# One product of 512 columns for two of 256 in the expert inputs of a float32 decoder step

## The chip, the cores and the metric

The kernel runs on one core of one Trainium2 chip. The metric is the device time of one execution in microseconds (us); less is better. The core has five engines: TensorE multiplies matrices (the profile shows its matmuls as PE and its weight loads as PEld), VectorE (DVE) and ScalarE (ACT) work on tiles elementwise, GpSimd (POOL) here mostly starts gathers, and SyncE (SP) starts the other transfers from memory. SBUF is the memory on the core, PSUM the memory that TensorE adds its products into; a PSUM tile here is one bank of 128 x 512 float32.

## The reference

A decoder trunk of two layers works on 256 prompt positions and 32 sample positions (8 sequences of 4), 288 rows of 1024 in all. The first layer mixes over time with RWKV-7, the second with differential attention. After each stands a "PEER" mixer, which holds this change: for every row it picks 16 experts of 16,384 for each of 8 heads, and an expert is a single neuron, one row of `u_tab` and one of `v_tab`.

```python
q = (xblk @ w_q + b_q).reshape(PEER_BLOCK, PEER_HEADS, 2, PEER_HALF)
sc = jnp.einsum('thcd,cnd->thcn', q, subkeys).astype(jnp.float32)
...
expert = i1 * PEER_NKEYS + i2
gate = jax.nn.softmax(s_sel, axis=-1)
h = jnp.einsum('td,thkd->thk', xblk, u_tab[expert])
act = (gate * jax.nn.gelu(h.astype(jnp.float32))).astype(xblk.dtype)
return jnp.einsum('thk,thkd->td', act, v_tab[expert])
```

## The kernel before, in words

For the 256 prompt rows the kernel does not gather experts: it computes all 16,384 of them, in 128 chunks of 128, and multiplies by a gate that is zero for those not picked. For the 32 sample rows it gathers the picked rows (64 gathers of 128 rows, 1 MB each).

**Split products.** Most products are taken on values split in two. ScalarE casts a float32 tile to float32r (the high part `wh`), VectorE subtracts it from the original (the low part `wl`); `split` does both, here in two halves of 512 columns. The activations have high and low parts too, `xH` and `xL` (`self.hl`), of 8 blocks `d` by 288 columns. `mm3` then makes three products for each block `d` of 128 inputs, all added into one PSUM tile: `wh` by `xH` (line 285), `wh` by `xL` (line 286), `wl` by `xH` (line 287).

**Hidden block.** `upto(n)` makes chunks of the first half of the mixer up to number n. For chunk c it loads 512 KB of `u` (transposed) into a `raw` tile, splits it (lines 263 and 264), runs `mm3` over 8 `d` on the 256 prompt columns, 24 matmuls into a PSUM tile `pu` (two such tiles take turns), and ScalarE applies the gelu from PSUM into `gel(c)` (line 1301). The first 23 chunks of a layer go another way (`direct`, line 1298): plain float32, no split, which TensorE runs as two instructions for each `d`. The 105 others of each layer take the split way.

**Output block.** The loop over c (line 1462) first calls `upto` for a few chunks ahead (line 1467: 31 chunks at the start, down to 8 ahead), then loads and splits 512 KB of `v` (`wload_rows`), multiplies gate and gelu on VectorE into `act` (line 1472), splits that into `ah` and `al`, and runs 24 matmuls (line 1491) of 256 columns into `pa`, four banks that gather the sum over all chunks. In the first part of the loop several output blocks stand between two hidden ones; from about c = 36 they alternate.

**Around them.** A gate table of half the experts is built before the loop and the other half in it, from c = 48 on: four VectorE instructions (lines 1401 to 1404), 32 small matmuls (lines 1411 and 1412) and ScalarE copies for 16 rows at a time, one such piece for each c. Between the chunks, a gather for the sample rows (line 1422) is followed by a dot product (line 1426) and a weighted sum (line 1430) on VectorE.

**Order.** The program is written chunk by chunk; a scheduler with a time model of its own arranges each engine's instructions, and each engine then works strictly in that order. Tiles named `raw` (three buffers), `wh` and `wl` (two each) are shared by hidden and output blocks in turn, so the cast for one block waits until TensorE has used the `wh` of two blocks before, and a load of `raw` waits until VectorE has subtracted the block three before.

Of the kernel before, what the change touches and what calls it, by code (L numbers as in the profile page):

```python
# [10 lines left out]
F32R = mybir.dt.float32r  # L11
# [10 lines left out]
NT, TP, TS = 288, 256, 32  # L22
# [120 lines left out]
class Yoco:  # L143
# [18 lines left out]
    def resident(self):  # L162

        p = self.ctx.enter_context(self.tc.tile_pool(name="hl", bufs=1, side="right"))
        self.xT = p.tile([128, 8, NT], F32, name="xT")
        self.ones = p.tile([128, 128], F32, name="ones")
        self.nc.gpsimd.memset(self.ones, 1.0 / 1024)
        self.one = p.tile([128, 128], F32, name="one")
        self.nc.gpsimd.memset(self.one, 1.0)
        self.alpha = p.tile([128, 128], F32, name="alpha")  # L170
        self.nc.scalar.activation(self.alpha, self.C["ident"], AF.Copy, scale=ALPHA)
        self.lnT = p.tile([128, 8, 8], F32, name="lnT")
        self.hl = p.tile([128, 8, NT], F32R, name="xH"), p.tile([128, 8, NT], F32R, name="xL")
        self.stream(self.ctx, *self.WS, "right")
        self.rp, self.att = p, None

# [102 lines left out]
    def mm3(self, ps, w, x, n, kb=8, ds=None):  # L279
        (wh, wl), (xh, xl) = w, x  # L280
        ps = ps[:, :n]
        blk = lambda t, d: t[d][:, :n] if isinstance(t, list) else t[:, d, :n]
        for d in ds or range(kb):
            h, l = wh[:, d * 128:(d + 1) * 128], wl[:, d * 128:(d + 1) * 128]
            self.nc.tensor.matmul(ps, h, blk(xh, d), start=d == 0, stop=False)  # L285
            self.nc.tensor.matmul(ps, h, blk(xl, d), start=False, stop=False)  # L286
            self.nc.tensor.matmul(ps, l, blk(xh, d), start=False, stop=d == kb - 1)  # L287

    def raw_load(self, src):

        w = self.raw()
        self.nc.sync.dma_start(w, src.rearrange("p b m -> p (b m)"))
        return w
# [965 lines left out]
    def peer(self, l, mean):  # L1259

        tc, nc, A, C = self.tc, self.nc, self.A, self.C
        V, S, T, G = nc.vector, nc.scalar, nc.tensor, nc.gpsimd
        uT, uv = A[f"uT{l}"], A[f"uv{l}"]
        with ExitStack() as es:
# [15 lines left out]
            def gel(c):  # L1280

                return early[:, c if c < A_ else (c - A_) % R_]
# [5 lines left out]
            def upto(n, direct=False):  # L1288


                while st["u"] < min(n, 128):
                    c = st["u"]
                    ps = self.psu()[:, :TP]
                    if direct:
                        w = self.raw(turn=True)
                        nc.sync.dma_start(w, uT[c].rearrange("p b m -> p (b m)"))
                        for d in range(8):
                            T.matmul(ps, w[:, d * 128:(d + 1) * 128], self.xT[:, d, :TP], start=d == 0, stop=d == 7)  # L1298
                    else:
                        self.mm3(ps, self.wload(uT[c]), self.hl, TP)  # L1300
                    S.activation(gel(c), ps, AF.Gelu_apprx_tanh)  # L1301
                    st["u"] += 1

            with tc.tile_pool(name="tk", bufs=1) as tk, ExitStack() as es2:
# [32 lines left out]
                for h in range(9):  # L1337
                    if h < 8:
                        self.proj(A[f"pq{l}"], self.hl, q_evac, ms=(2 * h, 2 * h + 1) if h else (), eng=G, pre=wq)
                    if h:  # L1340
                        for j in range(2):
                            self.tk_half(tk2, tt[j], qT, sk, h - 1)
                    upto(self.DIRECT.get(h, 0), True)
                    if h % 4 == 0 and h:
                        for j in range(2):
                            self.tk_pairs(tk2, tt[j], h - 4, 4)
                    if 1 <= h < 5:
                        self.ln_rest(4 * l, 2 * h - 2)
                        self.ln_rest(4 * l, 2 * h - 1)
                    if h == 6:  # L1350
                        with self.behind(last + after[1:]):
                            S.copy(self.io, C["iota"].unsqueeze(2).to_broadcast([128, 128, 2]))
                            S.copy(self.i16, C["iota"][:, :16].unsqueeze(2).to_broadcast([128, 16, 16]))
                            if not self.att:
                                self.attention_scalars()
                    if h == 4:
                        self.dbg(f"x1_{l}", self.xT)
                        xs4 = tk2.tile([128, 8, 4, TS], F32, name="xs4")
                        S.copy(xs4, self.xT[:, :, TP:].unsqueeze(2).to_broadcast([128, 8, 4, TS]))
                        for n in range(2):  # L1360
                            ps = self.psa()
                            for b in range(4):
                                T.transpose(ps[:, b * 128:(b + 1) * 128], xs4[:, 4 * n + b].rearrange("p r t -> p (r t)"), C["ident"])
                            S.copy(Xs[:, n * 512:(n + 1) * 512], ps)
                for j in (0, 1):
                    iw, gt = self.tk_decode(tk2, tt[j])
                    upto(self.DEC[j], True)
                    ps = self.psb()
                    ts = slice(j * 128, (j + 1) * 128)
                    for n, x in enumerate((iw[:, 0], iw[:, 1], gt.rearrange("p u k -> p (u k)"))):  # L1370
                        T.transpose(ps[:, n * 128:(n + 1) * 128], x, C["ident"])
                    S.copy(i1T[:, ts], ps[:, 0:128])
                    S.copy(i2T[:, ts], ps[:, 128:256])
                    g15 = tk2.tile([128, 128], F32, tag="g15", name=self.nm("g15"))
                    S.activation(g15, ps[:, 256:384], AF.Copy, scale=32768.0)
                    V.tensor_copy(gH[:, ts], g15)
                    V.tensor_sub(gL[:, ts], g15, gH[:, ts])
                upto(self.FIRST, True)
                self.ws = one
            self.hs = self.HG  # L1380
# [81 lines left out]
            for c in range(128):  # L1462
# [20 lines left out]
                if c == 127:  # L1483
                    ps = self.psb()[:, :TP]
                    for b in range(8):
                        T.matmul(ps[:, b * TS:(b + 1) * TS], accS[:, b * 128:(b + 1) * 128], C["rep"][:, :TS], start=True, stop=True)
                    x = self.xT[:, :, TP:]
# [9 lines left out]
            for n in range(4):  # L1497
                x = self.xT[:, 2 * n:2 * n + 2, :TP]
# [391 lines left out]
```

## Time and profile before

| | |
|---|---|
| median of three runs | 2329.24 us (2320.59 to 2331.36) |
| profiled execution | 2323.59 us |
| its span, first to last instruction | 2321.8 us |
| mean granted TensorE clock | 0.989 of full speed |
| TensorE / VectorE / ScalarE / GpSimd busy | 97% / 76% / 51% / 17% of the span |
| moved by DMA | 439.44 MB, mean 189 GB/s |

The span is the profiled execution's time from its first to its last instruction; 1.8 us lie around it. A line of instructions is named by its line of the kernel (L1491), by what it writes and reads (`pa<-ah,wh`), and by the shape; numbers behind the bar are busy us, mean ns of one, and the idle time of the engine before it with what ended it. A matmul's time in the records reaches from its start to the arrival of its result, so neighbours overlap.

### The profile page before, as it was taken

The numbers are of one execution on the slowest core, as the hardware profiler recorded it, in microseconds if no ns is written. First come the engines' busy times: TensorE is split into PE (matmuls) and PEld (weight loads), VectorE is DVE, ScalarE is ACT, GpSimd is POOL, SyncE is SP. The second block draws the span as 40 slices with busy tenths as digits, with TensorE's granted clock in tenths as the row PEclk, the third lists the DMA queues.
The fourth block names the chain that finished last, engine by engine and source line by source line (L and its number), as shares of the span: only waits on it lengthen the run. The fifth ranks groups of instructions, "written<-read, shape, count | busy, mean of one in ns | idle before, by whom it ended". The sixth has DMA issues, their size and how long they took to land. (4 is left out here: it accounts for less than half of the span.)

```text
span 2321.8 us, 49203 instructions
## 1 busy us (share of the span) xinstructions
PE 2253.4 (97%) x19296; PEld 2121.8 (91%) x19296; DVE 1759.4 (76%) x4125; ACT 1177.1 (51%) x2713; POOL 391.1 (17%) x424
## 2 busy tenths in 40 slices
PE   9989999999999999999999999999999999999998
PEld 6768889799999999999999888979999999999998
DVE  5758788977776987777785657897877797776776
ACT  3425453445455555544565666345545564554555
POOL 0323154000210210010013246100101021101101
PEclk9989999999999999999999999999999999999999
DMA  5222443245666567776746564325567656777673
GB/s 185 73 67 80 126 160 119 95 151 166 239 242 226 192 215 258 244 253 237 263 170 237 200 207 144 114 83 173 186 237 244 215 196 214 254 247 258 235 244 122
DMA packets 117624, 439.44 MB, mean 189 GB/s; under 512 B 14504, under 2 KB 18264, under 8 KB 108560
## 3 DMA queue, kind: packets, MB, share of 16 engines
q1 hardware_dynamic: 103216, 351.86, 44.8%
q0 software_dynamic: 14176, 84.44, 10.4%
q8 instruction: 151, 2.47, 0.4%
q14 instruction: 81, 0.66, 0.1%
HBM read 424.05 MB, written 5.94 MB: 185 GB/s over the span
## 5 line engine op out<-in xcount | busy, mean ns | idle before, releaser
L263 ACT CAST wh<-raw 128x512 fp32r<-128x512 f32 x1116 | 657.0, 617 | 696.0 <-PE pa L1491 223.7
L264 DVE TENSOR_TENSOR wl<-raw,wh 128x512 fp32r<-128x512 f32 x1052 | 704.0, 694 | 322.1 <-ACT wh L263 304.9
L1491 PE MATMUL pa<-al,wh 128*128 128x256 f32 x2048 | 569.7, 278 | 2.6 <-DVE al L264 2.5
L1491 PE MATMUL pa<-ah,wh 128*128 128x256 f32 x2048 | 568.1, 278 | 1.6 <-ACT ah L263 1.6
L1491 PE MATMUL pa<-ah,wl 128*128 128x256 f32 x2048 | 567.7, 277 | 0.6 <-DVE wl L264 0.4
L287 PE MATMUL pu<-xH,wl 128*128 128x256 f32 x1696 | 482.7, 285 | 15.8 <-DVE wl L264 15.0
L286 PE MATMUL pu<-xL,wh 128*128 128x256 f32 x1696 | 481.9, 284 | 0.0
L285 PE MATMUL pu<-xH,wh 128*128 128x256 f32 x1696 | 480.8, 284 | 0.9 <-ACT wh L263 0.9
L1491 PEld LDWEIGHTS pa<-al,wh 128*128 128x128 f32 x2048 | 386.1, 189 | 3.3 <-DVE al L264 3.2
L1491 PEld LDWEIGHTS pa<-ah,wh 128*128 128x128 f32 x2048 | 384.9, 188 | 2.9 <-ACT ah L263 1.8
L1491 PEld LDWEIGHTS pa<-ah,wl 128*128 128x128 f32 x2048 | 386.3, 189 | 1.2 <-DVE wl L264 1.2
L287 PEld LDWEIGHTS pu<-xH,wl 128*128 128x128 f32 x1696 | 321.4, 189 | 20.8 <-DVE wl L264 20.4
L285 PEld LDWEIGHTS pu<-xH,wh 128*128 128x128 f32 x1696 | 324.3, 191 | 1.7 <-ACT wh L263 1.5
L286 PEld LDWEIGHTS pu<-xL,wh 128*128 128x128 f32 x1696 | 323.2, 191 | 0.2 <-DVE xL L264 0.2
L285 PE MATMUL pa<-xH,wh 128*128 128x288 f32 x656 | 196.4, 302 | 0.3 <-ACT xH L263 0.3
L1422 POOL DMA_INDIRECT gt<-in_uv,ex x64 | 107.8, 1684 | 516.0 <-DVE accS L1430 489.9
L286 PE MATMUL pa<-xL,wh 128*128 128x288 f32 x656 | 193.9, 297 | 0.6 <-DVE xL L1113 0.5
L287 PE MATMUL pa<-xH,wl 128*128 128x288 f32 x656 | 192.8, 295 | 0.1
L1478 POOL COPY pace<-act 128x1 f32<-128x1 f32 x64 | 37.6, 588 | 887.8 <-DVE act L1472 846.3
L1298 PE MATMUL pu<-xT,raw 128*128 128x256 f32 x736 | 172.9, 386 | 0.0
L1298 PEld LDWEIGHTS pu<-xT,raw 128*128 128x128 f32 x736 | 136.6, 192 | 17.6 <-issue 1.0
L1301 ACT ACTIVATE gel<-pu 128x256 f32<-128x256 f32 x256 | 97.1, 379 | 75.4 <-PE pu L1298 75.2
(491 smaller groups left out, 3592.2 us busy)
## 6 DMA issues: line engine op xcount, KB each, us to landing
raw<-in_uT SPq DMA_DIRECT2D x256, 512.0 KB
raw<-in_uv SPq DMA_DIRECT2D x256, 512.0 KB
raw<-in_pq SPq DMA_DIRECT2D x32, 512.0 KB
raw<-in_wg SPq DMA_DIRECT2D x16, 512.0 KB
raw<-in_rw_w_k SPq DMA_DIRECT2D x8, 512.0 KB
raw<-in_rw_w_r SPq DMA_DIRECT2D x8, 512.0 KB
raw<-in_rw_w_v SPq DMA_DIRECT2D x8, 512.0 KB
raw<-in_rw_w_o SPq DMA_DIRECT2D x8, 512.0 KB
```

Source lines behind the costliest of these rows:

```text
L263: self.nc.scalar.copy(h, x)
L264: self.last = (eng or self.nc.vector).tensor_sub(l, x, h).ins
L285: self.nc.tensor.matmul(ps, h, blk(xh, d), start=d == 0, stop=False)
L286: self.nc.tensor.matmul(ps, h, blk(xl, d), start=False, stop=False)
L287: self.nc.tensor.matmul(ps, l, blk(xh, d), start=False, stop=d == kb - 1)
L1298: T.matmul(ps, w[:, d * 128:(d + 1) * 128], self.xT[:, d, :TP], start=d == 0, stop=d == 7)
L1301: S.activation(gel(c), ps, AF.Gelu_apprx_tanh)
L1422: G.indirect_dma_start(out=gt, out_offset=None, in_=uv, in_offset=bass.IndirectOffsetOnAxis(ap=ex[:, col:col + 1], axis=0))
L1478: with tc.issue_after(G.tensor_copy(pace, act[:, :1]).ins):
L1491: T.matmul(acc[b], w[:, b * 128:(b + 1) * 128], x, start=False, stop=c == 127 and b % 2 == 1 and w is vl)
```

## The change

The two tiles `xH` and `xL` become one tile `xHL`, in which the two parts of each `d` lie side by side; the old names are views of it. For the split hidden blocks, `mm_hidden` takes the place of `mm3`: `wh` meets the prompt columns of both parts in one product of 2 x 256 columns, which fills a whole PSUM bank (first half: sum over `xH`, second half: sum over `xL`), and `wl` by `xH` is added to the first half as before. The two halves are then added: ScalarE copies the second into `gel(c)`, VectorE adds the first to it, and the gelu works in place there.

```diff
-        self.hl = p.tile([128, 8, NT], F32R, name="xH"), p.tile([128, 8, NT], F32R, name="xL")
+        self.parts = p.tile([128, 8, 2, NT], F32R, name="xHL")
+        self.hl = self.parts[:, :, 0], self.parts[:, :, 1]
...
+    def mm_hidden(self, ps, wh, wl):
+
+
+        T, x = self.nc.tensor, self.parts
+        for d in range(8):
+            h, l = wh[:, d * 128:(d + 1) * 128], wl[:, d * 128:(d + 1) * 128]
+            T.matmul(ps.rearrange("p (n t) -> p n t", n=2), h, x[:, d, :, :TP], start=d == 0, stop=d == 7, skip_group_check=True)
+            T.matmul(ps[:, :TP], l, x[:, d, 0, :TP], start=False, stop=d == 7, skip_group_check=True)
...
-                    ps = self.psu()[:, :TP]
+                    both = self.psu()
+                    ps = both[:, :TP]
...
-                        self.mm3(ps, self.wload(uT[c]), self.hl, TP)
+                        self.mm_hidden(both, *self.wload(uT[c]))
+                        S.copy(gel(c), both[:, TP:])
+                        V.tensor_add(gel(c), ps, gel(c))
+                        ps = gel(c)
                     S.activation(gel(c), ps, AF.Gelu_apprx_tanh)
```

## Rows read from the trace of the kernel before

**Rows 1.** The page: busy time, share of the span, instructions.
```profile
PE 2253.4 (97%) x19296; PEld 2121.8 (91%) x19296; DVE 1759.4 (76%) x4125; ACT 1177.1 (51%) x2713; POOL 391.1 (17%) x424
```

**Rows 2.** Windows: busy PE, PEld, DVE, ACT, POOL; clock, DMA. 1844:1910 builds gates.
```profile
1755.00:1837.00 82.00, 81.95 (x703) 81.72 (x701) 57.74 (x102) 43.38 (x94) 5.78 (x7) 1.00 0.67 229
1844.00:1910.00 66.00, 66.00 (x802) 65.65 (x799) 65.64 (x109) 39.84 (x104) 14.03 (x5) 1.00 0.61 209
2020.00:2130.00 110.00, 109.94 (x941) 109.51 (x940) 80.87 (x144) 55.78 (x122) 13.28 (x14) 1.00 0.73 256
```

**Rows 3.** Timeline: a hidden block (24 matmuls), an output block (24), the next hidden one.
```profile
1814.63 0.28 PE L285 MATMUL pu<-xH,wh 128*128 128x256 f32 x1
...
1817.36 0.28 PE L287 MATMUL pu<-xH,wl 128*128 128x256 f32 x1
1817.48 0.28 PE L1491 MATMUL pa<-ah,wh 128*128 128x256 f32 x1
1817.49 0.19 PEld L1491 LDWEIGHTS pa<-al,wh 128*128 128x128 f32 x1
...
1820.23 0.28 PE L285 MATMUL pu<-xH,wh 128*128 128x256 f32 x1
```

**Rows 4.** Timeline of TensorE: plain f32 hidden blocks; a projection on 288 columns.
```profile
1489.78 19.16 PE L1298 MATMUL pu<-xT,raw 128*128 128x256 f32 x88
...
1476.62 0.29 PE L287 MATMUL pa<-xH,wl 128*128 128x288 f32 x1
...
1478.88 0.29 PE L286 MATMUL pa<-xL,wh 128*128 128x288 f32 x1
```

**Rows 5.** The page's groups on TensorE: busy us, mean ns, idle before.
```profile
L287 PE MATMUL pu<-xH,wl 128*128 128x256 f32 x1696 | 482.7, 285 | 15.8 <-DVE wl L264 15.0
L1298 PE MATMUL pu<-xT,raw 128*128 128x256 f32 x736 | 172.9, 386 | 0.0
```

**Rows 6.** Groups from 1837 to 1924 us; from 752 to 839 the same count.
```profile
L285 PE MATMUL pu<-xH,wh 128*128 128x256 f32 x104 | 30.3, 291 | 0.0
```

**Rows 7.** Groups of ScalarE and VectorE in the whole span.
```profile
L263 ACT CAST ah<-act 128x256 fp32r<-128x256 f32 x256 | 103.2, 404 | 1.7 <-DVE act L1472 1.5
L1301 ACT ACTIVATE gel<-pu 128x256 f32<-128x256 f32 x256 | 97.1, 379 | 75.4 <-PE pu L1298 75.2
L1843 DVE SCALAR_TENSOR_TENSOR xT<-xT,pa 128x288 f32<-128x288 f32 x14 | 6.4, 454 | 13.5 <-PE pa L287 13.5
```

**Rows 8.** Timeline of VectorE while gates are built.
```profile
1858.17 0.41 DVE L1472 TENSOR_TENSOR act<-G,gel 128x256 f32<-128x256 f32 x1
1858.51 1.28 DVE L264 TENSOR_TENSOR wl<-raw,wh 128x512 fp32r<-128x512 f32 x2
```

**Rows 9.** Chain that ended last, rounds with gates, first and last of 11: start, us.
```profile
1841.05 2.73 PE pa L1491 x24
...
1907.18 2.75 PE pa L1491 x24
```

**Rows 10.** Timelines of ScalarE and VectorE in an ordinary round.
```profile
1817.56 0.62 ACT L263 CAST wh<-raw 128x512 fp32r<-128x512 f32 x1 [1.35 <-PE pu L286]
1818.09 0.38 ACT L1301 ACTIVATE gel<-pu 128x256 f32<-128x256 f32 x1
...
1816.63 0.42 DVE L264 TENSOR_TENSOR al<-act,ah 128x256 fp32r<-128x256 f32 x1
1818.22 0.69 DVE L264 TENSOR_TENSOR wl<-raw,wh 128x512 fp32r<-128x512 f32 x1 [0.71 <-ACT wh L263]
```

**Rows 11.** Groups of VectorE from 1927 to 2251 us; 842 to 1165 has the same counts.
```profile
L1426 DVE CUSTOM_DVE_ANT_0 gt<-gt,Xs 128x1024 f32<-128x1024 f32 x20 | 24.4, 1220 | 4.6 <-DMA gt<-in_uv,ex 4.6
L1430 DVE SCALAR_TENSOR_TENSOR accS<-gt,hd,accS 128x1024 f32<-128x1024 f32 x19 | 24.3, 1279 | 0.0
L264 DVE TENSOR_TENSOR al<-act,ah 128x256 fp32r<-128x256 f32 x57 | 23.9, 419 | 0.1
```

**Rows 12.** The chain that ended last: a load beside a gather.
```profile
1727.30 7.50 DMA raw<-in_uT
```

## The prediction

> **What bounds the kernel now.** I read the page's busy line first, then the windows by stretch, then the order of time on TensorE. The busy line has TensorE at 97% of the span, VectorE at 76%, ScalarE at 51% [rows 1]. Such averages don't say which engine sets the pace, so the windows come next [rows 2]: in the two ordinary stretches of the loop over chunks (1755 to 1837 us, 2020 to 2130 us) TensorE is busy for 81.95 of 82.00 and 109.94 of 110.00 us, VectorE for 70% and 74%. In the stretch that also builds gates (1844 to 1910 us) TensorE has 66.00 of 66.00 and VectorE 65.64: there both are full. The reader should see two regimes: one in which VectorE has a quarter of its time to give, and one in which it has nothing.
>
> A busy TensorE says little about its speed, because the recorded matmuls (285 ns each in a hidden block) overlap [rows 5]. What counts is the distance between starts. In a hidden block (24 matmuls on `pu`) it runs from 1814.63 to 1817.48 us: 2.85 us, 119 ns a matmul, 356 ns for the three of one `d`. The output block on `pa` goes from 1817.48 to 1820.23: 2.75 us, 114 ns each [rows 3]. The granted clock is 1.00, so 2.4 GHz, at which 256 columns are 107 ns. A hidden matmul thus costs 12 ns more than its columns. Where one weight load feeds 512 column times, in the plain f32 blocks, 88 instructions take 19.16 us; without the 0.38 us tail of the last that is 216 ns each, 3 ns over their columns [rows 4]. The same three-product code on 288 columns has starts 133 ns apart (17 steps, 1476.62 to 1478.88), 13 ns over 120 [rows 4].
>
> TensorE hardly waits in these blocks: for the third product, 15.8 us in 1,696 [rows 5].
>
> **The change part by part.**
>
> *TensorE, removed and added.* 1,680 of the 1,696 matmuls of line 287 are hidden blocks of 8, so 210 blocks (the other 16 belong to the attention's output, 288 columns). A block falls from 24 matmuls to 16: per `d` one of 512 columns and one of 256. No column is saved: 768 before, 768 after. What can be saved is one instruction's surplus, and whatever weight loading sticks out behind a 256-column product and fits behind a 512-column one. No row has a 512-column product on these split tiles, so it gets bounds: 216 ns from the plain f32 blocks (same column time behind one load), and 232 ns from the 256- and 288-column rows (14 ns for 32 columns, so 113 for 256 more, on 119). The remaining product lies between 114 ns (output block) and 119 ns (hidden block). The pair is 330 to 351 ns against 356: it saves 5 to 26. I take 220 + 118 = 338, nearer the f32 row since it is the one with a load that has 512 columns to hide behind: 18 ns per `d`, 0.144 us a block.
>
> Two stretches of 87 us build gates, one per layer; each has 104 matmuls of line 285, so 13 blocks, 26 in all [rows 6]. The other 184 save 184 x 0.144 = 26.5 us (bounds 7 to 38).
>
> *ScalarE.* Each block gets a copy of 128x256 out of PSUM: 379 ns by the gelu that reads the same tile now. The gelu then reads SBUF, as the cast to `ah` does at 404 ns: 25 more [rows 7]. That is 0.40 us a block; ScalarE is busy for 43.38 of 82 us, and 39.84 of 66 [rows 2]. I cost it at nothing: TensorE's next block covers it. Without this cover it would be 210 x 0.40 = 84 us.
>
> *VectorE.* Each block gets an addition of 128x256, one operand from PSUM. Nearest rows: 0.41 us for `act` (256 columns, SBUF) [rows 8] and 454 ns for line 1843 (288 columns with PSUM) [rows 7]. In dense work the next instruction starts before the last one's record ends: `act` at 1858.17, its successor at 1858.51, so 0.34 us of the engine [rows 8]. In the ordinary stretches this takes VectorE from 70 to 76% or so and is covered by TensorE's blocks. In the gate stretches nothing covers it. There the round (ten from 1841.05 to 1907.18: 6.61 us each [rows 9]) is full on VectorE, so it grows by up to 0.34, and TensorE's saving is lost inside it: 26 x 0.34 = +8.8 us. Bounds: nothing, if VectorE's 0.36 us of idle in 66 and its gather work shift; 26 x 0.45 = 12 us if none of the overlap is had.
>
> *The wait that is new.* The addition waits for the copy, the copy for the block's last matmul, and the gelu for the addition. Now, when the hidden block ends (1817.48), ScalarE first does half a cast (1817.56), then the gelu (1818.09), then the second half; VectorE starts on that chunk's `wl` at 1818.22 [rows 10]. TensorE wants those weights at 1820.23 [rows 3]. A copy and an addition pushed into this order delay the second half by at most 0.38 + 0.34 us, and that half is wanted only halfway through the next hidden block, at 1821.65 or so. Slack exists, so I cost it at nothing here. Behind the waiting addition on VectorE stand the other `wl` half and the next `act`; behind the gelu on ScalarE stands a cast.
>
> Where a gather's sums stand in front (two instructions of 1.22 and 1.28 us), the slack is thinner: 20 gathers lie in each of the two long stretches after the gates [rows 11]. Also, a raw buffer is given back by that second `wl` half, so its next load is issued up to 0.34 us later, and loads beside a gather already take 7.50 us on the chain that ended last [rows 12]. Price: between nothing and 40 x 0.34 = 14 us. I take 4, since TensorE is idle for only 0.06 us in the 110 us after 2020, gathers and all [rows 2].
>
> *At no cost.* `xH` and `xL` become one tile with the two parts of a `d` side by side. Each user reads or writes one `d`, still 288 contiguous columns, so nothing else changes. `pu` keeps its two banks; a bank comes free one copy and one addition later, about 1.8 us into the next block, which lasts 2.7. Loads stay the same in number and size.
>
> *A rule that speaks against.* The hidden block's rows put 12 ns on each product beyond its columns, the f32 rows 3 ns on 512 [rows 3, 4]. The Trainium skill, "TensorE: Matmul & The Clock Gate", section "Wait — 56ns, not 53.3ns?", states a fixed cost of about 2.5 ns per warm matmul, downstream of decode. An estimate by that page: eight matmuls fewer are 20 ns a block, 184 x 0.020 = 3.7 us instead of 26.5, and the sum would end at +9.
>
> *Sum.* -26.5 + 8.8 + 4 = -13.7 us on the profiled execution's 2323.59, so 2309.9. That execution is 5.65 us under the median of the three runs, 2329.24. I apply the difference to the median: **2315.5, forecast 2315 us**.
>
> **The rivals.**
>
> *A. The full saving.* 26 ns per `d`, and the gate stretches lose half: -38 + 4.4 = -34, so 2295 us. For it: 216 ns is a measured distance for 512 column times. Against it: VectorE's 65.64 of 66.
>
> *B. Columns are all that counts.* The 512 product costs two of 256 (238 ns), or little under: 0 to -7 us on TensorE, then +8.8 and +4: 2335 to 2342 us. For it: the 288-column rows keep the same surplus over their columns as the 256-column ones, though their load has more time to hide. Against it: the f32 rows at 216. The fixed cost that the Trainium skill states leads here as well.
>
> *C. The addition stands in the way on VectorE (slower).* Place: ahead of `al` for the output block. `al` ends at 1817.05, and the load just ahead of its product starts at 1817.49, so the slack is 0.44 us [rows 3, 10], 0.30 after the shorter hidden block. A copy and an addition in this chain are 0.38 + 0.34 = 0.72. It decides from 0.30 us on; in full it costs 0.72 - 0.44 = 0.28 a round, in the 57 rounds of each long stretch after the gates [rows 11] 114 x 0.28 = +32. With +8.8 and -10 for the other 70 blocks: 2360 us. For it: the queues are in order, and every block gets the wait. Against it: the block's sum is ready when the output block begins, and `al` is made at its other end.
>
> **How the numbers follow.** A measurement of this kernel can tell about 0.5%, 11.6 us, from no change: 2317.6 to 2340.9 is "same". Chances: forecast 0.46 (its own range 2306 to 2326, two thirds of it under 2317.6), A 0.17, B 0.22, C 0.15. Faster: 0.30 + 0.17 = 0.47. Same: 0.16 + 0.17 = 0.33. Slower: 0.05 of B + 0.15 = 0.20. The range, 2293 to 2341, reaches just past A and over most of B; it leaves out C and a little on either side.
>
> **What would show it right or wrong.** In the profile after: starts within a hidden block alternate by about 220 and 118 ns, and the block takes 2.70 us (A: 2.64, B: 2.85). The gate round is 6.9 to 7.0 us with VectorE full and TensorE at about 95% (A: 6.6 to 6.8). In the ordinary stretches TensorE stays at 99%, and the round falls from 5.60 to 5.45 us. The forecast is wrong if the 512-column product is at or above 235 ns, if TensorE waits for `wl` or `al` outside the gate stretches by more than 0.1 us a round (C), or if the gate round stays at 6.61.

## The result and the profile after

The changed kernel takes 2345.71 us (median of six runs, 2341.36 to 2352.70); the kernel before, beside it, 2330.22. The ratio is 1.0083, interval 1.0063 to 1.0103: slower by 0.8%, and outside the predicted range. The profiled execution takes 2347.97 us, its span 2346.2, which is 24.4 more than before.

The page of the kernel after, busy time and the groups of the changed lines:

```profile
PE 2265.8 (97%) x17616; PEld 2040.0 (87%) x17616; DVE 1820.2 (78%) x4335; ACT 1259.7 (54%) x2923; POOL 368.4 (16%) x424
...
L296 PE MATMUL pu<-xHL,wh 128*128 128x512 f32 x1680 | 610.3, 400 | 4.1 <-ACT wh L264 4.0
...
L297 PE MATMUL pu<-xHL,wl 128*128 128x256 f32 x1680 | 483.5, 288 | 15.8 <-DVE wl L265 11.4
...
L1315 ACT ACTIVATE gel<-gel 128x256 f32<-128x256 f32 x210 | 88.0, 419 | 77.5 <-DVE gel L1313 76.5
```

A matmul's busy time says as little as before; starts count. The timeline of TensorE over a hidden block and the start of the output block behind it answers to [rows 3]:

```profile
1817.12 0.40 PE L296 MATMUL pu<-xHL,wh 128*128 128x512 f32 x1
1817.36 0.28 PE L297 MATMUL pu<-xHL,wl 128*128 128x256 f32 x1
1817.47 0.39 PE L296 MATMUL pu<-xHL,wh 128*128 128x512 f32 x1
1817.70 0.28 PE L297 MATMUL pu<-xHL,wl 128*128 128x256 f32 x1
...
1819.91 0.28 PE L1505 MATMUL pa<-ah,wh 128*128 128x256 f32 x1
...
1822.65 0.40 PE L296 MATMUL pu<-xHL,wh 128*128 128x512 f32 x1
```

The hidden block takes 2.79 us instead of 2.85, the output block 2.74 as before. The product of 512 columns takes 0.23 us, the other 0.12: over all undisturbed blocks the medians are 231 and 118 ns. The blocks' medians are 2.793 and 2.849 us, so 210 x 0.056 = 11.8 us are saved, and still the span grows. The windows of the three stretches of [rows 2], the middle one moved along with its gates, show TensorE idle for 0.6 to 0.8 us in each, where it was idle for 0.00 to 0.06, and VectorE still full in the gate stretch:

```profile
1755.00:1837.00 82.00, 81.39 (x587) 75.44 (x586) 61.87 (x117) 47.87 (x106) 8.49 (x7) 1.00 0.70 229
1859.00:1925.00 66.00, 65.21 (x686) 60.56 (x684) 65.34 (x113) 40.80 (x108) 6.71 (x5) 1.00 0.62 202
2020.00:2130.00 110.00, 109.39 (x776) 100.32 (x774) 87.02 (x164) 65.27 (x146) 11.84 (x13) 1.00 0.71 244
```

To see where the time goes, I took from each profiled execution the start of the output blocks of chunks 9, 16, 36, 48, 64 and 127 in both layers and summed the layers. Between 9 and 16 the experts of the sample rows are picked on VectorE (`sample_topk`), 48 to 64 holds the gates, 64 to 127 is the long stretch after them. The kernels below the second row are explained further down. Differences to the kernel before, in us:

| kernel | 9 to 16 | 16 to 36 | 48 to 64 | 64 to 127 | span |
|---|---|---|---|---|---|
| before (itself) | 62.9 | 168.9 | 214.4 | 682.8 | 2321.8 |
| after | +6.2 | -6.5 | +12.4 | +14.0 | +24.4 |
| no_sum | -1.6 | +8.8 | -0.6 | +0.9 | +8.9 |
| halves256 | +5.7 | -5.1 | +5.7 | +27.2 | +33.6 |
| extra_add | -2.6 | +7.6 | +30.1 | +10.6 | +50.5 |
| extra_copy | +0.3 | -0.6 | -0.4 | -2.1 | -4.0 |
| pool_add | +6.6 | -0.2 | +23.3 | +33.2 | +68.2 |
| gate_old | +6.4 | -5.2 | +1.4 | +20.6 | +26.4 |
| before_ng | -1.8 | -8.1 | +1.9 | +3.0 | +4.6 |
| after_ng | +6.3 | -9.0 | +0.1 | -3.7 | +2.3 |
| no_sum_ng | +1.0 | -9.0 | +0.0 | -3.7 | -7.3 |
| before_nosums | +0.3 | -12.7 | -3.3 | -12.1 | -27.1 |
| after_nosums | +5.7 | -2.7 | -3.4 | -0.4 | +0.2 |
| after_sums | +6.4 | -14.9 | +10.1 | -21.0 | -22.9 |

Each row is one execution. The kernel before's lies 6.6 us under its median, the kernel after's 2.3 over: the spans differ by 24.4 us, the medians by 15.5. Three kernels that take the same time as the one before (extra_copy, and before_pad and before_shift, described below) differ from its row by at most 1.5, 5.7, 0.8 and 2.2 us in the four stretches; a difference of that size says nothing.

The loss of the kernel after is thus in three places: the picking, the gates, and the long stretch. In the last, 112 hidden blocks and 126 output blocks at their undisturbed medians (2.849 and 2.745 us before, 2.793 and 2.741 after) would take 665.0 and 658.2 us. So 6.8 should have been saved there, and 14.0 were lost.

The chain that ended last shows one round of that stretch in the kernel after (start, us, what):

```profile
2009.29 1.09 DVE accS L1444
2010.38 0.62 DVE wl L265
...
2011.04 0.39 PE pu L297
...
2012.12 0.24 PE pu L296
2012.37 0.02 issue
2012.39 0.63 ACT wh L264
2013.02 0.02 issue
2013.04 0.69 DVE wl L265
2013.73 0.33 DVE gel L1313
2014.07 0.61 DVE wl L265
2014.68 0.02 issue
2014.70 6.84 DMA raw<-in_uv
```

A gather's sum makes `wl` late, TensorE waits for it inside its block, and the new addition (0.33 us) stands on the chain between the two halves of the next `wl`. Only when the second half is done is the raw buffer given back; its next load starts at 2014.70, beside a gather, and takes 6.84 us.

### The profile page after: what moved, and what is told of

Read it like the earlier page. It is cut to its first block, busy times and chain, and to the rows that moved or that the text cites. A ratio compares the mean times of both kernels' runs of the same rounds, so it can differ in the third digit from the quotient of the medians.

```text
span 2346.2 us, 46219 instructions
## 1 busy us (share of the span) xinstructions
PE 2265.8 (97%) x17616; PEld 2040.0 (87%) x17616; DVE 1820.2 (78%) x4335; ACT 1259.7 (54%) x2923; POOL 368.4 (16%) x424
## 5 line engine op out<-in xcount | busy, mean ns | idle before, releaser
L296 PE MATMUL pu<-xHL,wh 128*128 128x512 f32 x1680 | 610.3, 400 | 4.1 <-ACT wh L264 4.0
L297 PE MATMUL pu<-xHL,wl 128*128 128x256 f32 x1680 | 483.5, 288 | 15.8 <-DVE wl L265 11.4
L296 PEld LDWEIGHTS pu<-xHL,wh 128*128 128x128 f32 x1680 | 319.5, 190 | 67.2 <-ACT wh L264 5.2
L297 PEld LDWEIGHTS pu<-xHL,wl 128*128 128x128 f32 x1680 | 320.1, 191 | 39.2 <-DVE wl L265 37.3
L286 PE MATMUL pa<-xHL,wh 128*128 128x288 f32 x656 | 197.3, 304 | 1.2 <-ACT xHL L1122 0.9
L287 PE MATMUL pa<-xHL,wh 128*128 128x288 f32 x656 | 195.0, 299 | 1.8 <-DVE xHL L1123 1.6
L288 PE MATMUL pa<-xHL,wl 128*128 128x288 f32 x656 | 193.5, 296 | 0.1
L1436 POOL DMA_INDIRECT gt<-in_uv,ex x64 | 101.7, 1589 | 492.6 <-DVE accS L1444 470.6
L1492 POOL COPY pace<-act 128x1 f32<-128x1 f32 x64 | 20.7, 323 | 958.2 <-DVE act L1486 920.5
L1309 PEld LDWEIGHTS pu<-xT,raw 128*128 128x128 f32 x736 | 136.7, 192 | 17.8 <-issue 1.0
L1315 ACT ACTIVATE gel<-gel 128x256 f32<-128x256 f32 x210 | 88.0, 419 | 77.5 <-DVE gel L1313 76.5
L287 PEld LDWEIGHTS pa<-xHL,wh 128*128 128x128 f32 x656 | 124.4, 190 | 4.1 <-DVE xHL L1123 3.7
L286 PEld LDWEIGHTS pa<-xHL,wh 128*128 128x128 f32 x656 | 123.2, 189 | 4.5 <-issue 1.8
```

The source lines that it names most:

```text
L296: T.matmul(ps.rearrange("p (n t) -> p n t", n=2), h, x[:, d, :, :TP], start=d == 0, stop=d == 7, skip_group_check=True)
L297: T.matmul(ps[:, :TP], l, x[:, d, 0, :TP], start=False, stop=d == 7, skip_group_check=True)
L1436: G.indirect_dma_start(out=gt, out_offset=None, in_=uv, in_offset=bass.IndirectOffsetOnAxis(ap=ex[:, col:col + 1], axis=0))
```

## The experiments

Each kernel ran against the kernel before on its own chip, so ratios are compared.

**First: is it VectorE's time?** Theory V: the addition's 0.34 us on an engine that is full. Rivals: S, the time on ScalarE or the longer way from a block to its gelu; O, another order of instructions.

no_sum, the kernel after without its copy and addition (the sum over `xL` is made and left out of the result):

```diff
-                        S.copy(gel(c), both[:, TP:])
-                        V.tensor_add(gel(c), ps, gel(c))
-                        ps = gel(c)
```

> The changed kernel without copy and addition: the gelu reads the first half of the bank from PSUM, so the products of wh with the low parts are made but left out of the result. Theory V (the loss is VectorE's 0.34 us for each addition): only the shorter hidden blocks are left, 210 x 0.06 us = 12.6 us faster than before, about 2318 us, and the gate stretches end without the 6 us of extra stall. Theory S (the loss is the wait of copy, addition and gelu on each other, whichever engine): the same here. Theory O (the loss comes from another order of instructions that any edit of this place brings): no faster than before, 2330 us or more.

halves256, three products of 256 columns as before, but into two halves that are added:

```diff
+            T.matmul(ps[:, :TP], h, xh[:, d, :TP], start=d == 0, stop=False, skip_group_check=True)
+            T.matmul(ps[:, TP:], h, xl[:, d, :TP], start=False, stop=d == 7, skip_group_check=True)
+            T.matmul(ps[:, :TP], l, xh[:, d, :TP], start=False, stop=d == 7, skip_group_check=True)
```

> The kernel before with the old three products of 256 columns, but the products with the low part summed in the second half of the bank, then copy and addition as in the changed kernel. It does the change's evacuation without its 512-column product. Theories V and S: slower than the changed kernel by the 12.6 us that the products save, about +28 us on before, 2358 us. If the 512-column product itself did harm (a rival to both), this one is faster than the changed kernel, below 2345 us.

extra_add, the kernel before with an idle addition (extra_copy: `S.copy(junk, gel(c))` in its place):

```diff
                     S.activation(gel(c), ps, AF.Gelu_apprx_tanh)
+                    if not direct:
+                        junk = dp.tile([128, TP], F32, tag="junk", name=self.nm("junk"), bufs=1)
+                        V.tensor_add(junk, gel(c), gel(c))
```

> The kernel before plus one VectorE addition of 128x256 for each split hidden block, on the finished gelu tile and into a tile that nobody reads: VectorE's time alone, with nothing waiting for it. Theory V: most of the evacuation's price, +20 to +28 us, 2350 to 2358 us, with a stall of some 6 us at the end of each gate stretch. Theory S: under +8 us.

> The kernel before plus one ScalarE copy of 128x256 for each split hidden block into a tile that nobody reads: ScalarE's time alone. Theory V: within 5 us of before. Theory S, in the form that ScalarE's 0.4 us a block is the price: +10 to +25 us.

Measured: no_sum 2327.61 us, 0.9996 (0.9978 to 1.0014); halves256 2351.57, 1.0094 (1.0069 to 1.0119); extra_add 2371.0, 1.0184 (1.0155 to 1.0213); extra_copy 2329.36, 0.9999 (0.9982 to 1.0016). ScalarE's time is free, which rejects that half of S. halves256 came out 6 us under the 2358 that V and S had. no_sum has the shorter blocks and gains nothing, as O had it and V and S had not: what it saves goes to waits. extra_add lost more than the 20 to 28 us of V, and most of it in the gates (+30.1), not in the long stretch. There the chain (its shares over 1890 to 1990 us of extra_add) hangs on a gather:

```profile
by line: DMA gt<-in_uv,ex 35.7%; PE pa L1494 19.2%; DVE wl L264 8.2%; PE pu L287 7.7%; PE pu L286 7.2%; PE pu L285 7.2%; DVE o L1405 3.9%; issue 3.1%; PE pb L1415 3.0%; PE pb L1414 2.8%; DVE ol L1404 2.5%; DVE oh L1406 2.5%; DVE accS L1433 
```

The instruction on GpSimd that starts this gather is the place:

```profile
1882.36 18.70 POOL L1425 DMA_INDIRECT gt<-in_uv,ex  x1 [14.74 <-DVE accS L1433]
...
1908.92 1.23 DVE L1429 CUSTOM_DVE_ANT_0 gt<-gt,Xs 128x1024 f32<-128x1024 f32 x1 [8.70 <-DMA gt<-in_uv,ex]
```

It lasted 18.70 us (at most 2.72 in the kernel after, 5.21 before). VectorE worked without a gap until 1900.22, when it lacked this gather, and the instruction ended 0.8 us later. Two more of 18.71 and 18.37 us, from 771.27 and 826.63, ended in the same way in the gates of the first layer. What held them up is not shown: in the kernel after such starts take 1.0 to 1.5 us in the gates of the first layer, beside VectorE at work without a gap for 29 us and more. VectorE waits 48.5 us for gathers in extra_add and 22.4 in the kernel before. So a good part of the 43 us is gathers that start late, and the run is no price for an addition's time.

**Second: the addition elsewhere, and the gates alone.** pool_add moves it off VectorE; gate_old keeps the old products for chunks 55 to 71; the pads give each `d` 320 columns in place of 288, so that every `d` lies at the same distance from a multiple of 256 bytes (160 bytes in the program, where the expectation has it on a multiple).

```diff
-                        V.tensor_add(gel(c), ps, gel(c))
+                        two = dp.tile([128, TP], F32, tag="two", name=self.nm("two"), bufs=2)
+                        S.copy(two, ps)
+                        G.tensor_add(gel(c), two, gel(c))
...
+                        if 55 <= c < 72:
+                            self.mm3(ps, self.wload(uT[c]), self.hl, TP)
...
+        self.hl = [p.tile([128, 8, 320], F32R, name=x)[:, :, :NT] for x in ("xH", "xL")]
```

> The changed kernel with the addition taken from VectorE: ScalarE copies both halves out of PSUM and GpSimd adds them. VectorE has no new work, but ScalarE has a copy more and the chain is longer. Theory V: the stalls at the gate stretches' ends go, and the time falls to 2318 to 2328 us. Theory S: no better than the changed kernel, 2345 us or more.

> The changed kernel, but chunks 55 to 71 of each layer, whose hidden blocks stand in or beside the gate stretch, take the old three products and no addition. Theory V, with the gate stretch as its main place: 2 x 6 us less than the changed kernel, less 34 x 0.06 us of lost saving, about 2335 us. Theory S (a price in every block): 34 of 210 blocks, so about 4 us less, 2341 us.

> The kernel before with 320 columns kept for each d of xH and xL instead of 288, of which 288 are used: every d then starts at a multiple of 256 bytes. If the start address makes a hidden matmul 119 ns where an output matmul on aligned tiles has 114: 5040 x 5 ns, 25 us faster, 2305 us. If not: 2330 us, starts 119 ns apart as before.

> The changed kernel with 320 columns kept for each part instead of 288. If start addresses make the 512-column product 231 ns: it falls to about 222, and the kernel to 2330 us. If not: 231 ns and 2346 us.

Measured: pool_add 2385.13, 1.0239 (1.0215 to 1.0264); gate_old 2341.59, 1.0049 (1.0030 to 1.0068); before_pad 1.0001 (0.9983 to 1.0019) with starts 119 ns apart; after_pad 1.0102 (1.0075 to 1.0128) with 230 ns. Theory V missed on pool_add: with no addition on VectorE the kernel is slower still. GpSimd's addition is long, and the gelu waits for it 115.6 us in all (groups of pool_add):

```profile
L1315 POOL TENSOR_TENSOR gel<-two,gel 128x256 f32<-128x256 f32 x210 | 210.1, 1001 | 923.0 <-ACT two L1314 902.2 <-DVE act L1488 20.8
L1317 ACT ACTIVATE gel<-gel 128x256 f32<-128x256 f32 x210 | 87.9, 418 | 115.7 <-POOL gel L1315 115.6
```

So the way from block to gelu seems to count too (the other half of S), though the gathers also start on GpSimd, and no run parts its additions from them. gate_old came out at the 2341 of S, but not by a price in every block: it removes the loss in the gates (+1.4 for +12.4) and gives half of it back later (+20.6 for +14.0).

**Third: the gathers.** The `_ng` kernels leave out the gathers and their sums (the `if c in when` and `if c in use` parts of the loop); extra_free is extra_add with `V.tensor_add(junk, self.xT[:, 0, :TP], self.xT[:, 1, :TP])`.

> Leaves out the gathers for the sample rows and the sums over them (the sample rows' share of the result stays empty); otherwise the kernel before. It is the base for the two runs beside it. If TensorE paces the kernel before and the gathers are hidden, it is 0 to 15 us faster than before (the stalls of TensorE that loads and sums beside gathers cause, about 6 to 15 us in the records); if they cost more, the time they cost shows here.

> The kernel after without gathers and their sums (left out of the result as in the run beside it). Theory V (the change loses where VectorE is full, which is the gate stretch and the rounds with a gather): without gathers the 12.6 us that the hidden blocks save stand against +11 to 13 us of the two gate stretches and up to +6 of the sample top-k rounds, so it lies 0 to +8 us above the base. Rival W (the addition costs in every round, as a wait between the blocks): it lies 14 to 20 us above the base, as the kernels do with gathers.

> The kernel after without the copy and the addition (the product of the high weights with the low activations is left out of the result), and without gathers and their sums. Theory L (with gathers the 12.6 us that the shorter hidden blocks save are eaten by raw loads that come late beside the gathers): 10 to 13 us under the base. Rival O (the scheduler's other order of the instructions, or something in every round, eats them): within 4 us of the base, as the pair with gathers.

> The kernel before with an idle VectorE addition of 128x256 for each split hidden block, as in the earlier run with such an addition, but from the residual tile, which is ready from the start, so that it waits for no gelu. If that run's +43 us are VectorE's time alone, it is +35 to +50 us again. If much of it came from standing behind the gelu in VectorE's order, it is under +25 us.

Measured: before_ng 2324.91, 0.9961 (0.9944 to 0.9978); after_ng 2321.15, 0.9943 (0.9926 to 0.9960); no_sum_ng 2311.15, 0.9903 (0.9885 to 0.9921); extra_free 2366.5, 1.0140 (1.0121 to 1.0160). Without gathers the change is not slower (-3.8 us), and without the addition the whole saving shows (-13.8 for 11.8), which speaks against O as a price in every round. extra_free tells little: its additions ran where VectorE came to them first, all before 1645 us, and 34 of the 43 us in its profile lie ahead of the output block of chunk 9 in the two layers.

One warning on these three: their output blocks are longer, 2.87 us instead of 2.74, as the chain of before_ng shows:

```profile
2049.92 2.87 PE pa L1484 x24
...
2055.66 2.87 PE pa L1484 x24
```

256 x 0.13 = 33 us are in all three alike. They are compared with one another only; and the longer rounds give VectorE more room, so they don't settle whether the sums or the transfers of a gather matter.

**Fourth: sums or transfers.** The `_nosums` kernels keep the gathers and leave out the sums (`if c in use`); after_sums does the sums on a still tile (`return still` for the gather); after_pool moves the second sum off VectorE:

```diff
-                V.scalar_tensor_tensor(accS, gt[:, 1024:], hd[:, col:col + 1], accS, op0=OP.mult, op1=OP.add)
+                S.activation(gt[:, 1024:], gt[:, 1024:], AF.Copy, scale=hd[:, col:col + 1])
+                G.tensor_add(accS, gt[:, 1024:], accS)
```

> Leaves out the sums over the gathered rows on VectorE, and keeps the gathers (the sample rows' share of the result stays empty). Otherwise the kernel before; base of the run beside it. Between 2320 and 2335 us, since neither sums nor gathers cost the kernel before more than some 9 us together.

> The kernel after, with the sums left out and the gathers kept. Theory V (VectorE's time for the sums and for the addition together is what costs): within -8 to +3 us of the base beside it, as without gathers (-3.8). Theory L (the transfers beside the raw loads cost it): 10 us or more above the base.

> The kernel after, with the sums done on a still tile of zeros, and without the gathers (the sample rows' share of the result stays empty). Theory V: 2338 to 2347 us, near the kernel after, since VectorE has all its work. Theory L: 2319 to 2328 us, as without gathers and sums (2321.2), since no transfer stands beside the loads. In between: both are needed, the late release of a raw buffer by VectorE and a slow load after it.

> The kernel after, whole, but the weighted sum over a gather's rows (1.28 us on VectorE) is a scaling on ScalarE and an addition of 128x1024 on GpSimd (about 4 us by the 1001 ns of 256 columns there). Theory V: half of the sums leaves VectorE, so it lands half way or further from 2345 to 2321: 2322 to 2335 us, perhaps under the kernel before. Theory L: within 5 us of the kernel after. Rival: GpSimd's work holds its own gathers back or slows VectorE, then it is slower than the kernel after.

Measured: before_nosums 2301.26, 0.9889 (0.9864 to 0.9914); after_nosums 2318.01, 0.9958 (0.9939 to 0.9976); after_sums 2302.86, 0.9897 (0.9871 to 0.9923); after_pool 2412.41, 1.0361 (1.0333 to 1.0389). Output blocks are 2.74 us again, so these compare with the rest. before_nosums was expected at 2320 to 2335 us and came out far under that; the longer output blocks of before_ng had hidden what gathers and sums cost. V predicted after_nosums near its base; it is 16.7 us above, as theory L (the transfers beside the raw loads) had it. after_sums fell under the ranges of both, furthest from V's. The sums cost both kernels about the same, 26 us without the change, 29 with it (1.0083 - 0.9958 = 0.0125 of 2330). Taking the transfers away and leaving VectorE all its sums takes 43 us off the kernel after (1.0083 - 0.9897). No run has the kernel before with its sums and without transfers, so these 43 us are not all the change's. The long stretch tells more, in the shares of the chain over 1985 to 2265 us: before, after, after_nosums, after_sums and before_nosums, one fence each.

```profile
by line: PE pa L1491 33.7%; DMA raw<-in_uv 16.0%; PE pu L287 11.4%; PE pu L286 10.8%; PE pu L285 10.6%; DVE wl L264 8.1%; DVE gt L1426 2.8%; issue 1.8%; ACT wh L263 1.7%; DVE accS L1430 1.4%; DVE al L264 1.2%; DVE act L1472 0.3%; ACT gel L1
```

```profile
by line: PE pa L1505 35.2%; PE pu L296 20.6%; DMA raw<-in_uT 13.1%; PE pu L297 12.7%; DVE wl L265 8.7%; DVE accS L1444 5.0%; DMA raw<-in_uv 2.4%; ACT wh L264 2.0%; DVE gt L1440 0.8%; issue 0.6%; DVE gel L1313 0.5%; DVE act L1486 0.3%; DVE a
```

```profile
by line: PE pa L1502 43.8%; PE pu L296 23.3%; DMA raw<-in_uv 17.1%; PE pu L297 11.8%; DVE wl L265 2.0%; ACT wh L264 1.6%; issue 0.4%; ACTq L264 0.1%
```

```profile
by line: PE pa L1505 48.0%; PE pu L296 29.3%; PE pu L297 14.8%; DMA raw<-in_wp 2.3%; DVE wl L265 1.1%; DVE xT L1083 1.0%; ACT wh L264 0.6%; issue 0.6%; PE pb L1516 0.6%; POOL v L1109 0.3%; ACT sq L1087 0.3%; DVE gt L1515 0.2%; PE pb L1115 0
```

```profile
by line: PE pa L1488 46.9%; PE pu L286 14.8%; PE pu L287 14.6%; PE pu L285 14.5%; DMA raw<-in_wp 2.2%; DVE wl L264 1.2%; DVE xT L1073 1.0%; issue 0.7%; ACT wh L263 0.6%; PE pb L1499 0.6%; DVE xL L1113 0.4%; PE pb L1105 0.4%; POOL v L1099 0.
```

Raw loads of `uT` and `uv` are on the chain in the first three (16%, 15.5%, 17.1%): gathers are transferred there, and VectorE has the sums, the addition or both. They are on it neither in after_sums, which has all of VectorE's work and no transfers, nor in before_nosums, which has all transfers and neither sums nor addition. (The loads of `wp` belong to what follows the loop, which ends before 2250 us in these two.) The windows from 1985 to 2245, inside all five loops and in the same order, say the same for TensorE:

```profile
1985.00:2245.00 260.00, 259.13 (x2198) 256.88 (x2198) 189.60 (x338) 133.48 (x292) 32.76 (x31) 1.00 0.72 249
1985.00:2245.00 260.00, 256.12 (x1805) 233.99 (x1805) 201.86 (x381) 150.17 (x335) 27.34 (x30) 1.00 0.70 243
1985.00:2245.00 260.00, 257.12 (x1833) 237.88 (x1832) 166.32 (x320) 148.62 (x321) 23.11 (x30) 1.00 0.74 249
1985.00:2245.00 260.00, 260.00 (x1906) 244.42 (x1905) 209.51 (x397) 154.88 (x343) 2.60 (x14) 1.00 0.62 191
1985.00:2245.00 260.00, 260.00 (x2239) 260.00 (x2238) 160.99 (x284) 133.01 (x280) 22.56 (x28) 1.00 0.72 249
```

It is idle for 0.87, 3.88 and 2.88 us, and not at all in the last two. Over both layers, the time of the long stretch above the 665.0 or 658.2 us of undisturbed blocks (some small products of the last chunk in it) is 17.8 us before, 38.6 after, 24.2 in after_nosums, 3.6 in after_sums and 5.7 in before_nosums. So the loss there needs both, transfers and more work on VectorE beside the loads; either alone costs next to nothing.

The gates answer the other way: +10.1 with the sums and no transfers, -3.4 with transfers and no sums, where the base without sums has -3.3. There it is VectorE, with the sums and the addition together. after_pool fell to its rival: GpSimd's sums (2.43 us each) wait for ScalarE, and gathers stand behind them; it didn't find a faster kernel.

**Fifth: the place of the tiles.** In the `_ng` kernels a small tile was gone, and so `ah` and `al` lay 64 bytes higher in the program; `wh` and `wl` lay where they were. It is neither the transfers nor the sums: after_sums and before_nosums have 2.74 us. before_shift and after_shift move the activations' parts by 64 bytes and all that lies below by 128:

```diff
+        p.tile([128, 16], F32, name="skip0")
         self.alpha = p.tile([128, 128], F32, name="alpha")
...
+        p.tile([128, 16], F32, name="skip1")
         self.stream(self.ctx, *self.WS, "right")
```

> The kernel before, with xH and xL 64 bytes further down in SBUF (a pad of 64 bytes on either side, so that the other tiles move by 128). Theory P (the 119 ns of a hidden product against 114 in the output block come from where the moving tile lies): starts in the hidden block 113 to 115 ns apart, the block 2.74 us instead of 2.85, 190 blocks x 0.11 = 20 us less where TensorE paces: 2303 to 2315 us for 2325 to 2330. Rival Q (the surplus belongs to the kind of block, or to the alternation of tiles): 119 ns, no change of the time.

> The kernel after, with xHL 64 bytes further down in SBUF in the same way. Theory P: the product of 512 columns takes 219 to 222 ns instead of 231, the one of 256 113 to 115, a hidden block 2.66 us instead of 2.79; time 2320 to 2340 us for 2340 to 2346, since the late loads beside the gathers and the full VectorE eat a part. Against the run beside it, it is then still slower, by 10 to 30 us. Rival Q: 231 ns and 2340 to 2346 us.

Measured: before_shift 2329.84, 1.0012 (0.9994 to 1.0030); after_shift 2361.12, 1.0138 (1.0110 to 1.0166). Theory P falls in its form: hidden blocks of before_shift take 2.83 us, some 2.80 (2.85 before), and the output blocks, whose tiles moved by a whole 128 bytes, went from 2.74 to 2.83, a quarter of them to 2.72. In after_shift they are 2.83 and 2.82, and the 512-column product takes 235 ns. Q falls as well, since place alone moved both kinds of blocks. Which distances matter stays open.

## Why the prediction was wrong

**TensorE, the term that was mis-sized.** The pair was taken at 220 + 118 = 338 ns; it is 231 + 118 = 349. The step that failed is the choice "nearer the f32 row": the upper bound, 232, worked out from the 256- and 288-column rows, was right to 1 ns. 119, 133 and 231 ns for 256, 288 and 512 columns lie on 7 ns + 0.4375 ns a column (7 + 224 = 231). On these tiles the surplus goes with the columns, and halving the instructions removes little of it. This was rival B's mechanism, at 231 instead of 238. The estimate by the Trainium skill, "TensorE: Matmul & The Clock Gate", section "Wait — 56ns, not 53.3ns?", of about 2.5 ns per instruction saved, was too low: 356 - 349 = 7 ns per `d`. Its fixed cost alone also doesn't give the 18 ns over 213 that the 512-column product shows. Saved: 11.8 us instead of 26.5 for 184 blocks, or 30 for 210.

**Gates: the mechanism right, the form not.** 8.8 us was predicted, 12.4 measured. VectorE is full there (65.34 of 66), and without the gather's sums, or with the old products, the loss is gone. But the round did not grow to 6.9 us: by the starts of the output blocks most gate rounds take 6.58. VectorE falls behind, and the debt is paid at the end: in the second layer the last pieces of the gate table begin 2.9 us further from the first (83.9 us for 81.0 before, by the starts of `o`, one of the four VectorE instructions of a piece), and the one round from chunk 62 to 63 takes 15.9 and 15.7 us in the two layers, where it took 9.9. In it TensorE waited 2 us for `ol`, and the granted clock then fell to 0.50 (1.2 GHz) for 6.8 us, which it did not before:

```profile
1934.50:1941.30 6.80, 6.48 (x61) 5.01 (x58) 6.80 (x11) 2.76 (x9) 0.00 (x0) 0.50 0.07 13
```

The waits are the larger part: in after_pad the clock fell in the first layer alone, and the stretches from 48 to 64 are 6.3 and 5.0 us longer than before. "The gate round stays at 6.61" was named as a sign of being wrong; it stayed, and the loss came all the same.

**The rounds with a gather: priced at 4, cost 20.8.** Beside TensorE's term this is the largest miss, 17 us. The long stretch is 14.0 us longer and should have been 6.8 shorter. The prediction had the place (a buffer given back later, a load beside a gather), and bounded it by 40 x 0.34 = 14 as if each delay were passed on once. What the runs showed in its place: with transfers and VectorE's sums or addition together, a raw load stands on the chain and TensorE waits; without transfers the kernel after loses nothing there. Shorter hidden blocks alone lose their saving here (no_sum +0.9 with gathers; no_sum_ng 6.7 under its base). The reason given for the small price, that TensorE was idle for 0.06 us after 2020, was read from one window; in the whole stretch from 1985 to 2265 it was idle for 0.87 us, and loads made up 16% of the chain. Idle time also hides waits, since a matmul's record is longer than the distance to the next start: by the starts, products of the two kinds of blocks came 3.9 us late from 1985 to 2245.

**The rounds that pick the sample's experts: not looked at, cost 6 us.** All kernels with an addition between block and gelu lose 5.4 to 8.1 us there against their base, on VectorE or GpSimd, with gathers or without; those without such an addition lose nothing (no_sum -1.6, extra_add -2.6) or 2.8 (no_sum_ng over its base). The traces show an output block that waits for `al`, and another order on VectorE. After, then before:

```profile
1674.52 1.22 DVE L1416 TENSOR_TENSOR o<-i2T,io 128x2048 f16<-128x2048 f16 x1
...
1676.80 0.42 DVE L265 TENSOR_TENSOR al<-act,ah 128x256 fp32r<-128x256 f32 x1
1677.28 0.58 PE L1505 MATMUL pa<-al,wh 128*128 128x256 f32 x1 [2.83 <-DVE al L265]
```

```profile
1658.86 0.42 DVE L264 TENSOR_TENSOR al<-act,ah 128x256 fp32r<-128x256 f32 x1
1659.33 0.58 PE L1491 MATMUL pa<-al,wh 128*128 128x256 f32 x1 [1.24 <-DVE al L264]
...
1665.82 1.22 DVE L1402 TENSOR_TENSOR o<-i2T,io 128x2048 f16<-128x2048 f16 x1
```

In all kernels with that addition, pool_add's on GpSimd too, this `o` of the first piece of the gate table stands ahead of the `al`, in both layers; in all others it stands behind. So here it is O, the order that the scheduler chose once the addition was there, and not VectorE's 0.34 us; no run moved that piece alone. **ScalarE at nothing** was right (extra_copy 0.9999). **Rival C** (the addition ahead of `al`) does not show in the long stretches: by the waits of the kernel after, the output blocks' products wait for `al` 3 times, 5.9 us in all, two of them in the picking just told, where C wanted 0.28 us in each of 114 rounds. The undisturbed round is 5.53 us, just the two blocks.

**Open.** Why the stretch from 16 to 36 got 6.5 us shorter: over the runs it lies between 14.9 under and 8.8 over the kernel before, and it is 5 us or more shorter in halves256 and gate_old too, as if the picking's loss were partly paid back there. Why a raw load beside a gather is on the chain more often with an addition: the round shown at 2009 to 2015 gives the link (addition, second `wl` half, load), but no run took away that link alone. What held up the start of three gathers in extra_add.

No version that computes the whole result was found to beat the kernel before.

## What to carry to other kernels

An instruction count is no price: before merging two products, look at whether their surplus over the columns is fixed or grows with them; two column counts in the same trace tell it. In a kernel whose mean engine is full to 97%, a saving on it is only worth what loads, and an engine that is full in some stretch, leave of it: price each stretch for itself, the short ones too. Work put between a block and the buffer that it frees can be paid in load time where transfers compete, not in its own 0.34 us. And where a scheduler orders the engines, compare the order before and after: one small instruction can move a larger one ahead of what TensorE waits for.

## What was not expected of the hardware

The same 24 products took 2.74, 2.82 or 2.87 us, at full clock and with no wait, by where their tiles lay in SBUF: a small tile that is left out can move a block by 5%. An instruction that starts a gather on GpSimd lasted 18.4 to 18.7 us in three places of extra_add, each time until 0.8 to 0.9 us after VectorE had run out of work; the other 61 took 1.0 to 6.1 us. A load of 512 KB takes 3.6 to 3.7 us from issue to landing without gathers (all loads of after_ng from 1940 to 2250 us):

```profile
raw<-in_uv SPq DMA_DIRECT2D x55, 512.0 KB, 3.7
raw<-in_uT SPq DMA_DIRECT2D x54, 512.0 KB, 3.6
```

Beside one it took 6.84 us in the round above. The change's addition of 128x256 takes 417 ns on VectorE, and 1001 ns on GpSimd in pool_add.
